# A fused decoder step on one Trainium2 core: the input projection of blocks 2 to 4 in products of 512, and a closer step distance in the last block

## The chip, the cores and the metric

The kernel runs on one core of one Trainium2 chip. The core has a matrix engine (TensorE: PE, with its weight load PEld), a vector engine (VectorE: DVE), a scalar engine (ScalarE: ACT), GpSimd (POOL), a queue engine that only issues transfers (SyncE: SP), and 16 DMA engines between main memory and the on-chip memory. PE writes its results into PSUM banks of 128 partitions by 512 fp32 columns. The metric is device time in microseconds, as a median over runs.

## The reference, cut to what matters

One layer of a decoder: 2048 prompt tokens and 64 sampled tokens pass a shared input projection, two groups of attention heads (FoX and mLSTM), an output projection and an MLP. The change is in the prompt's part of the first line:

```python
z = jnp.einsum('bsd,dc->bsc', x, w_in)          # 2112 tokens, 1024 -> 3600 columns
fq, fk, fv = z[..., 0:512], z[..., 512:1024], z[..., 1024:1536]      # FoX q, k, v
conv = conv_b + sum(xpad[:, j:j + S] * conv_w[j] for j in range(4))  # over the mLSTM q and k columns
mv, og = ..., jax.nn.sigmoid(z[..., OFF_M_O:] + b_og)                # mLSTM v and output gate
(C, n, m), h = lax.scan(_mlstm_chunk, init, chunks of q, k, v, gates)
```

All matrices are fp32. The kernel splits each operand into a high part in the PE's fp32r format and a low remainder, and forms each product as high x high, low x high and high x low.

## The kernel before, in words

**Phases.** Phase A is the input projection (about 0 to 875 us in the profile) with the mLSTM recurrence and a part of the sampled tokens' attention beside it. Phase B is the FoX attention of the prompt, phase O the output projection, phase C the MLP.

**Blocks.** Phase A goes through four blocks of tokens (`BLKS`): block 1 has the 64 sampled tokens and prompt tiles 0 to 3, blocks 2 to 4 have four tiles of 128 tokens each. In the code they are `bi` 0 to 3. A block's x, transposed to 8 slices (k) of 128 model dimensions by tokens, is split by `x_turn` into the tiles `xh0`, `xl0` (the first 256 or 320 tokens) and `xh1`, `xl1` (the last 256). `block_a(bi)` then runs five stages in this order:

- mLSTM v: `natural` twice, 256 columns of `w_in` at a time. For each tile, 24 products (`mm3` for 8 values of k: three products each) with 128 tokens as the stationary operand and 256 columns of weights as the moving one.
- mLSTM q and k, with the short convolution: 8 groups (j) of 128 columns. The weights are stationary, the tokens move: two PSUM banks (i), 24 products of 256 tokens each, and ACT copies each bank into `qi`.
- output gate: `natural` twice, the gate formed in `sink`, stored to `dog`.
- FoX q and k: 8 groups of two banks, as for mLSTM q and k, each half stored through a tile `st`.
- FoX v: `natural` twice, stored to `v_prompt`. In between, `turn_first` loads the next block's x, and splits its first tile ahead of the last tile's products of this block. In block 4 `begin_b` loads the first keys and queries of phase B.

Weights come by `wload`: for each 256 columns two transfers of 512 KB, split by ACT (high part, `whi`) and DVE (low part, `wlo`).

**What runs beside.** After each tile or bank the code calls `tick(us)`, which adds the stated time to two counters. As soon as `macc` holds more than `PACE_M` = 2.3 us, one step of the recurrence (`m_block`, for block 1's sampled tokens `m_sample`) is issued; as soon as `acc` holds more than `PACE_A` = 5.6 us, one step of the sampled attention. A step of `m_block` is a few small products with the DVE, ACT and POOL work on their results, which the next step needs. What is left of the recurrence after block 4 is issued at the end of phase A, in a loop. A framework then places every instruction in its engine's queue by its own estimate of times, so the order on an engine differs a little from that of the code.

**Names.** `pm` is the projection's PSUM tile (4 banks), `mm` and `mn` those of the recurrence, `sQ`, `sT`, `sO` those of the sampled attention, `pS` the scores of phase B. `kn`, `qn`, `nl`, `vn` are phase B's keys, queries, forget sums and values, `ks` the split keys, `wr<-w_o` the output projection's weights, which phase B asks for ahead of phase O.

Of the kernel before, what the change touches and what calls it, by code (L numbers as in the profile page):

```python
# [10 lines left out]
F32 = mybir.dt.float32  # L11
# [3 lines left out]
OP = mybir.AluOpType  # L15
# [6 lines left out]
PACE_B = float('inf')  # L22
PACE_C = 4.93
PACE_M = 2.3
D = 1024
S = 2048
NB = 8
# [25 lines left out]
def body(ctx, tc, I, O, stages):  # L53
# [99 lines left out]
    def split_hi(dst, src, scale=1.0):  # L153
        last["ACT"] = A.activation(dst, src, AF.Copy, scale=scale)  # L154

    def split_lo(dst, src, hi, eng=None):
        r = (eng or V).tensor_tensor(dst, src, hi.bitcast(F32), op=OP.subtract)  # L157
        if eng is None:
            last["DVE"] = r
        return r  # L160
# [133 lines left out]
    v_out = lambda t: (O["v_sample"].rearrange("l b t h d -> (l b t) (h d)") if t == 16  # L294
                       else O["v_prompt"].rearrange("l b s h d -> (l b s) (h d)")[t * 128:(t + 1) * 128])

    xT = {}

    def geom(bi):
        blk = BLKS[bi]  # L300
        pre = 64 if bi == 0 else 0
        off = {}
        o = 0
        for t in blk:
            off[t] = o
            o += tok_n(t)
        return blk, pre, off
# [8 lines left out]

    def x_turn(bi, t):

        blk, pre, off = geom(bi)
        i = int(off[t] >= pre + 256)  # L320
        if len(xT.setdefault(bi, [])) == i:
            w = 256 if i else 320
            xT[bi].append((pa.tile([128, 8, w], F32R, name=f"xh{i}"), pa.tile([128, 8, w], F32R, name=f"xl{i}")))
        n = tok_n(t)
        xn = xns.pop(t)[:, :8 * n].rearrange("p (k c) -> p k c", k=8)
        (xh, xl), s = xcol(bi, t)
        split_hi(xh[:, :, s], xn)
        split_lo(xl[:, :, s], xn, xh[:, :, s])

    def xcol(bi, t):  # L330

        blk, pre, off = geom(bi)
        o = off[t]
        i = int(o >= pre + 256)
        o -= i * (pre + 256)
        return xT[bi][i], slice(o, o + tok_n(t))

    def gate_stream(bi):
        blk, pre, off = geom(bi)
# [118 lines left out]
    def block_a(bi):  # L458
# [3 lines left out]
        def natural(sink, *cols, hook=None, after=None):  # L462
            wh, wl = W0.pop() if W0 else wload(*cols)
            for i, t in enumerate(blk):
                if hook:
                    hook(i)
                m = tok_n(t)
                ps = ppa.tile([128, 512], F32, name="pm", tag="pm", bufs=4)[:m, :wh[0].shape[1]]
                (xh, xl), s = xcol(bi, t)
                for k in range(8):  # L470
                    mm3(ps, xh[:, k, s], xl[:, k, s], wh[k], wl[k], k == 0, k == 7)
                sink(t, m, ps)
                if after:
                    after(i)
                tick(2.6)

        def stage(ps, m, n):
            st = pa.tile([128, 256], F32, name="st", bufs=4)[:m, :n]
# [25 lines left out]
        for j in range(8):  # L504
            if j % 2 == 0:
                wh, wl = wload((C_QK + j * 128, 256))
            cs = slice((j % 2) * 128, (j % 2) * 128 + 128)
            qi = pa.tile([128, 515], F32, name="qi", bufs=2)
            V.tensor_copy(qi[:, 0:3], hist[:, j])
            if pre:  # L510
                qs = pa.tile([128, 8, 11], F32, name="qs", bufs=2)
                V.tensor_copy(qs[:, :, 0:3], scT[:, j])
            for i in range(2):
                xh, xl = xT[bi][i]
                w = 256 + (pre if i == 0 else 0)
# [6 lines left out]
                A.copy(qi[:, 3 + i * 256:259 + i * 256], ps[:, w - 256:])  # L522
# [24 lines left out]
        if bi == 3:  # L547
            SY.dma_start(O["conv_prompt"], hist)
        yield 1
        for i in range(2):  # L550
            def sink(t, m, ps, i=i):
                r = tok_r(t)
                cs = slice(i * 256, (i + 1) * 256)
                st = pa.tile([128, 256], F32, name="st", bufs=4)[:m]
                V.tensor_tensor(st, ps, bog[:m, cs], op=OP.add)
                A.activation(st, st, AF.Tanh, scale=0.5)
                V.scalar_tensor_tensor(st, st, 1.0, nwh[:m, cs], op0=OP.add, op1=OP.mult)
                SY.dma_start(dog[r:r + m, cs], st)
            natural(sink, (C_O + i * 256, 256))
        gated.add(bi)  # L560

        for j in range(8):
# [7 lines left out]
            for i in range(2):  # L570
                xh, xl = xT[bi][i]
                w = 256 + (pre if i == 0 else 0)
                ps = ppa.tile([128, 512], F32, name="pm", tag="pm", bufs=4)[:, :w]
                for k in range(8):
                    mm3(ps, wh[k][:, cs], wl[k][:, cs], xh[:, k, :w], xl[:, k, :w], k == 0, k == 7)
                tick(w * 0.01)
                if w == 320:
                    for a in range(4):
                        V.tensor_scalar(qr[:, :, (j % 2) * 4 + a], ps[a * 32:a * 32 + 32, 0:64].rearrange("p (b t) -> p b t", t=8), scale, None, op0=OP.mult)
# [4 lines left out]
                st = pa.tile([128, 256], F32, name="st", bufs=4)  # L584
                A.activation(st, ps[:, w - 256:], AF.Copy, scale=scale)
                a = t0 + i * 256
                SY.dma_start(O["k_prompt"][jj * 128:(jj + 1) * 128, a:a + 256] if c else dq[jj, :, a:a + 256], st)
# [3 lines left out]
        for i in range(2):  # L591
            def sink(t, m, ps, i=i):
                d = v_out(t)[:, i * 256:(i + 1) * 256]
                (A if bi == 3 and i == 1 else SY).dma_start(d, stage(ps, m, 256))
# [9 lines left out]
            def b_first(n, i=i):  # L604
                if i == 1 and n == 0:
                    begin_b()
            natural(sink, (1024 + i * 256, 256), hook=b_first if bi == 3 else turn_first)

    dgs_s = drm.tile([4, 8], F32, name="dgs_s")

# [1392 lines left out]
```

## Time and profile before

| | |
|---|---|
| median of 3 runs | 3212.57 us (3210.7 to 3214.76) |
| the profiled execution's own time | 3215.55 us |
| its span, first to last instruction | 3213.8 us |
| PE busy, share of the span | 3124.1 us, 97% |
| DVE, ACT, POOL busy | 2082.2, 1446.8, 910.1 us |
| mean granted TensorE clock | 0.990 |
| DMA packets, mean | 732.75 MB, 228 GB/s |

Busy time is the union of an engine's instructions. A matmul's end is modelled and consecutive matmuls overlap, so a product's own duration is longer than the step to the next one; the step is read from the starts in the timeline. "Idle before" is the time an engine stood still just before an instruction, and the releaser is what ended it.

### The profile page before, as it was taken

What the parts mean: (1) busy time and instruction counts of PE and PEld (TensorE: products, weight loads), DVE (VectorE), ACT (ScalarE), POOL (GpSimd) and SP (SyncE); (2) the same over time, 40 slices, a digit from 0 to 9 for tenths busy, and PEclk for the clock granted to TensorE, in tenths of its full rate; (3) what the DMA queues carried; (4) which work ended last, traced back from release to release, by engine and by line L of the source; (5) the groups of instructions that cost most, each with busy time, mean ns of one, the idle gap of its engine ahead of it and who ended that gap; (6) DMA issues with size and microseconds to landing.
All of it is one profiled execution on the core that took longest, in us unless ns stands there. A gap on an engine that the chain in (4) does not pass through costs nothing. (4 is left out here: it accounts for less than half of the span.)

```text
span 3213.8 us, 57419 instructions
## 1 busy us (share of the span) xinstructions
PE 3124.1 (97%) x21597; PEld 2538.6 (79%) x21597; DVE 2082.2 (65%) x5046; ACT 1446.8 (45%) x2678; POOL 910.1 (28%) x973
## 2 busy tenths in 40 slices
PE   9999999999999999999999999999999999899998
PEld 8998998998867677677777777777767777698886
DVE  6856556465488788534556568556675665766667
ACT  4343344334378677412444445343444444344442
POOL 0121323423333333376333323334333211000000
PEclk9999999999999999999999999999999999999999
DMA  5565766867676866687887869878879866643231
GB/s 190 151 211 166 264 218 226 273 219 260 219 251 186 193 168 145 214 297 259 308 292 271 308 237 322 317 256 313 291 260 340 288 210 204 211 163 131 100 123 63
DMA packets 339340, 732.75 MB, mean 228 GB/s; under 512 B 63608, under 2 KB 177656, under 8 KB 338168
## 3 DMA queue, kind: packets, MB, share of 16 engines
q1 hardware_dynamic: 251928, 414.61, 39.8%
q0 software_dynamic: 83520, 304.12, 27.1%
q10 hardware_dynamic: 3616, 10.36, 0.9%
q8 instruction: 171, 2.80, 0.3%
q14 instruction: 105, 0.86, 0.1%
HBM read 676.13 MB, written 86.38 MB: 237 GB/s over the span
## 5 line engine op out<-in xcount | busy, mean ns | idle before, releaser
L157 DVE TENSOR_TENSOR wl<-wr,wh 128x1024 fp32r<-128x1024 f32 x300 | 365.7, 1222 | 246.1 <-ACT wh L154 207.1
L154 ACT ACTIVATE wh<-wr 128x1024 fp32r<-128x1024 f32 x300 | 315.4, 1055 | 330.7 <-PE py L165 140.0
L163 PE MATMUL ph<-x1h,wh 128*128 128x512 f32 (+1 forms) x1280 | 455.2, 356 | 0.0
L164 PE MATMUL ph<-x1l,wh 128*128 128x512 f32 (+1 forms) x1280 | 453.5, 354 | 0.2 <-DVE x1l L157 0.2
L165 PE MATMUL ph<-x1h,wl 128*128 128x512 f32 (+1 forms) x1280 | 451.5, 355 | 0.4 <-DVE wl L157 0.2
L1720 POOL DMA_INDIRECT kT<-cache_k,idxK x256 | 276.4, 1080 | 533.7 <-PE sQ L1743 468.6
L163 PE MATMUL py<-wh,hh 128*128 128x512 f32 x900 | 358.8, 403 | 10.4 <-DVE y L1369 6.4
L164 PE MATMUL py<-wl,hh 128*128 128x512 f32 x900 | 354.4, 395 | 0.7 <-issue 0.7
L165 PE MATMUL py<-wh,hl 128*128 128x512 f32 x900 | 351.9, 395 | 0.7 <-DVE hl L157 0.4
L1369 DVE TENSOR_TENSOR y<-y,py 128x512 f32<-128x512 f32 x410 | 276.8, 681 | 106.5 <-PE py L165 80.3
L163 PE MATMUL pm<-xh,whi 128*128 128x256 f32 (+1 forms) x1024 | 298.5, 292 | 0.0
L164 PE MATMUL pm<-xl,whi 128*128 128x256 f32 (+1 forms) x1024 | 294.5, 288 | 0.0
L165 PE MATMUL pm<-xh,wlo 128*128 128x256 f32 (+1 forms) x1024 | 293.6, 287 | 0.5 <-issue 0.5
L1831 POOL DMA_INDIRECT vt<-cache_v,idxV x164 | 179.1, 1092 | 386.8 <-PE sO L1855 315.1
L163 PEld LDWEIGHTS ph<-x1h,wh 128*128 128x128 f32 x1280 | 241.2, 188 | 40.2 <-issue 8.5
L165 PEld LDWEIGHTS ph<-x1h,wl 128*128 128x128 f32 x1280 | 240.6, 189 | 36.7 <-issue 3.7
L164 PEld LDWEIGHTS ph<-x1l,wh 128*128 128x128 f32 x1280 | 241.5, 189 | 35.0 <-issue 3.7
L163 PE MATMUL pm<-whi,xh 128*128 128x256 f32 (+2 forms) x816 | 237.0, 291 | 9.8 <-ACT whi L154 7.2
L164 PE MATMUL pm<-wlo,xh 128*128 128x256 f32 (+2 forms) x816 | 232.6, 285 | 0.8 <-DVE wlo L157 0.6
L165 PE MATMUL pm<-whi,xl 128*128 128x256 f32 (+2 forms) x816 | 232.3, 285 | 0.8 <-issue 0.8
L163 PEld LDWEIGHTS py<-wh,hh 128*128 128x128 f32 x900 | 169.4, 189 | 65.2 <-issue 25.1
L157 DVE TENSOR_TENSOR wlo<-wra,whi 128x1024 fp32r<-128x1024 f32 (+1 forms) x112 | 141.6, 1266 | 102.0 <-ACT whi L154 95.5
(364 smaller groups left out, 6806.7 us busy)
## 6 DMA issues: line engine op xcount, KB each, us to landing
wr<-w SPq DMA_DIRECT2D x200, 512.0 KB
wra<-w_in SPq DMA_DIRECT2D x104, 512.0 KB
wr<-dw SPq DMA_DIRECT2D x96, 512.0 KB
dw<-w POOLq DMA_DIRECT2D x48, 512.0 KB
Rb<-dR SPq DMA_DIRECT2D x128, 128.0 KB
kT<-dw SPq DMA_DIRECT2D x28, 512.0 KB
kT<-w SPq DMA_DIRECT2D x25, 512.0 KB
xn<-xp_t SPq DMA_DIRECT2D x16, 512.0 KB
```

The source lines that it names most:

```text
L154: last["ACT"] = A.activation(dst, src, AF.Copy, scale=scale)
L157: r = (eng or V).tensor_tensor(dst, src, hi.bitcast(F32), op=OP.subtract)
L163: T.matmul(ps, wh, xh, start=first, stop=False, skip_group_check=shared)
L164: T.matmul(ps, wh, xl, start=False, stop=False, skip_group_check=shared)
L165: last["PE"] = T.matmul(ps, wl, xh, start=False, stop=stop, skip_group_check=shared)
L1369: V.tensor_tensor(y, y, ps, op=op)
L1720: G.indirect_dma_start(out=piece(n), out_offset=None, in_=ck, in_offset=IO(ap=idxK[:, b, j // 2, j % 2:j % 2 + 1], axis=0))
L1831: vx["last"] = G.indirect_dma_start(out=vt.rearrange("p f c -> p (f c)"), out_offset=None, in_=cv, in_offset=IO(ap=idxV[:, b, (kt % 4) * 4 ...
```

## The change

In blocks 2 to 4 a block's x lies in one pair of tiles `XX` (`xh`, `xl`, 4608 columns), tile by tile, each tile as 8 slices of 128 tokens. mLSTM q and k and FoX q and k take all 512 tokens of a block in one product, whose moving operand is then four runs of 128 tokens. Output gate and FoX v are formed by a new function `wide`: four PSUM banks are open at once, one for each tile, the weights come in four pieces q of 2 slices by 512 columns, and each product moves 512 columns, as two runs of 256 with a step between them. mLSTM v and all of block 1 stay as they were. The ticks of the two kinds of stages add up to the same. In block 4 `PACE_M` becomes 2.05 us after the output gate. FoX v of block 4 is stored from the ACT queue for all four tiles.

```diff
+PACE_M3 = 2.05
...
-    xT = {}
+    XX = []
...
     def x_turn(bi, t):
-        blk, pre, off = geom(bi)
-        i = int(off[t] >= pre + 256)
-        if len(xT.setdefault(bi, [])) == i:
-            w = 256 if i else 320
-            xT[bi].append((pa.tile([128, 8, w], F32R, name=f"xh{i}"), pa.tile([128, 8, w], F32R, name=f"xl{i}")))
+        if not XX:
+            XX.extend(pa.tile([128, 4608], F32R, name=x) for x in ("xh", "xl"))
...
+    def xrun(bi):
+        if bi:
+            return [(512, [X[:, 0:4096].rearrange("p (t k c) -> p k t c", t=4, k=8) for X in XX])]
+        return [(w, [X[:, a:a + 8 * w].rearrange("p (k c) -> p k c", k=8) for X in XX]) for a, w in ((0, 320), (2560, 256))]
...
+        def wide(sink, c0, hook=None):
+            banks = [ppa.tile([128, 512], F32, name="pm", tag="pm", bufs=4) for _ in blk]
+            at0, at1 = (w_at[((c0 + i * 256, 256),)] for i in range(2))
+            for q in range(4):
+                wr = pa.tile([128, 4 * 272], F32, name="wra", bufs=2)[:, :1024]
+                SY.dma_start(wr.rearrange("p (s e) -> p s e", s=2),
+                             dap(I["w_in"], at0 + q // 2 * 131072 + q % 2 * 512, [[1024, 128], [at1 - at0, 2], [1, 512]]))
...
+                split_hi(wh, wr)
+                split_lo(wl, wr, wh)
+                wh, wl = (x.rearrange("p (s k c) -> p k s c", s=2, k=2) for x in (wh, wl))
+                for i, t in enumerate(blk):
+                    xh, xl = xcol(bi, t)
+                    for k in range(2):
+                        mm3(banks[i].rearrange("p (s c) -> p s c", s=2), xh[:, 2 * q + k], xl[:, 2 * q + k], wh[:, k], wl[:, k],
+                            q == k == 0, q == 3 and k == 1)
+                    if hook:
+                        hook(q, i)
+                    if q == 3:
+                        st = (pa.tile([128, 512], F32, name="sa", tag="ac", bufs=2) if i % 2 else
+                              pa.tile([128, 512], F32, name="sq", tag="qi", bufs=2))
+                        sink(t, banks[i], st)
+                    tick(1.3)
...
-            for i in range(2):
-                xh, xl = xT[bi][i]
-                w = 256 + (pre if i == 0 else 0)
+            for w, (xh, xl) in xrun(bi):
                 ps = ppa.tile([128, 512], F32, name="pm", tag="pm", bufs=4)[:, :w]
+                pv = ps.rearrange("p (t c) -> p t c", t=4) if w == 512 else ps
                 for k in range(8):
-                    mm3(ps, wh[k][:, cs], wl[k][:, cs], xh[:, k, :w], xl[:, k, :w], k == 0, k == 7)
+                    mm3(pv, wh[k][:, cs], wl[k][:, cs], xh[:, k], xl[:, k], k == 0, k == 7)
                 tick(w * 0.01)
...
+        if bi == 3:
+            macc[2] = PACE_M3
...
+        def at(q, i):
+            if bi == 3:
+                if (q, i) == (2, 0):
+                    begin_b()
+            elif q < 3 and i == 0:
+                x_load(BLKS[bi + 1][q])
+            elif (q, i) == (3, 0):
+                x_turn(bi + 1, BLKS[bi + 1][0])
+                x_load(BLKS[bi + 1][3])
+
+        if bi:
+            wide(v_store, 1024, at)
```

Three places show what stands in the queues. The first is PE among block 4's FoX q groups, where half a step of the recurrence (`mn`, products of chunk values `va` and state `Cs`) stands between the projection's products (`pm`). Before, at the change from the first half of the block's tokens (`xh0`, `xl0`) to the second (`xh1`, `xl1`):

```order
L164 MATMUL pm_10094<-xl0_8442,whi_9976 128x256
L165 MATMUL pm_10094<-xh0_8441,wlo_9977 128x256
L719 MATMUL mn_10119<-va_9576,Wm_9579 128x129
L720 MATMUL mn_10119<-Cs_8404,qa_9581 128x129
L719 MATMUL mn_10119<-va_9576,Wm_9579 128x129
L720 MATMUL mn_10119<-Cs_8404,qa_9581 128x129
L163 MATMUL pm_10138<-xh1_8512,whi_9970 128x256
L164 MATMUL pm_10138<-xl1_8513,whi_9970 128x256
```

After, at the change from one group of 128 columns to the next (the tiles `xh` and `xl` hold all 512 tokens):

```order
L165 MATMUL pm_8447<-xl_148,whi_8354 128x512
L166 MATMUL pm_8447<-xh_147,wlo_8355 128x512
L778 MATMUL mn_8472<-va_8089,Wm_8092 128x129
L779 MATMUL mn_8472<-Cs_7119,qa_8094 128x129
L778 MATMUL mn_8472<-va_8089,Wm_8092 128x129
L779 MATMUL mn_8472<-Cs_7119,qa_8094 128x129
L778 MATMUL mn_8483<-va_8089,Wm_8092 128x129
L779 MATMUL mn_8483<-Cs_7119,qa_8094 128x129
L778 MATMUL mn_8483<-va_8089,Wm_8092 128x129
L779 MATMUL mn_8483<-Cs_7119,qa_8094 128x129
L164 MATMUL pm_8548<-xh_147,whi_8538 128x512
L165 MATMUL pm_8548<-xl_148,whi_8538 128x512
```

Each group of 24 products of 256 has become part of one of 24 products of 512, and two steps (the two `mn` halves) now stand together where before one stood, with 24 products of 256 between it and the next.

The second place is PE at the end of phase A: the last products of FoX v in block 4, the last of the recurrence (`mn<-va,kw`, and the transposes `mm<-ident,hh` of its result), and the first scores of phase B (`pS`). Before:

```order
L163 MATMUL pm<-whi,xh_8512 128x256
L164 MATMUL pm<-wlo,xh_8512 128x256
L165 MATMUL pm<-whi,xl_8513 128x256
L728 MATMUL mn<-va,kw 128x129 x4
L634 MATMUL mm<-ident,hh 128x128 x4
L974 MATMUL pS<-ks_11274,qh 128x256
L975 MATMUL pS<-ks_11274,ql 128x256
L974 MATMUL pS<-ks_11274,qh 128x256
```

After:

```order
L164 MATMUL pm<-whi,xh 128x512
L165 MATMUL pm<-wlo,xh 128x512
L166 MATMUL pm<-whi,xl 128x512
L693 MATMUL mm<-ident,hh 128x128 x4
L164 MATMUL pm<-whi,xh 128x512
L165 MATMUL pm<-wlo,xh 128x512
L166 MATMUL pm<-whi,xl 128x512
L164 MATMUL pm<-whi,xh 128x512
L165 MATMUL pm<-wlo,xh 128x512
L166 MATMUL pm<-whi,xl 128x512
L1033 MATMUL pS<-ks_9340,qh 128x256
L1034 MATMUL pS<-ks_9340,ql 128x256
```

The transposes stood behind the last product of the projection; now six products of 512 stand behind them, and the last `mn` products stand earlier still.

The third place is the SP queue at the same end, where the results of the recurrence (`C_prompt`, `n_prompt`, `dmix`) and phase B's first loads are issued. Before:

```order
L637 DMA dmix<-ot 128x4x128
L925 DMA nl_11273<-dnl 128x512
L926 DMA vn_11272<-v_prompt 128x4x64
L741 DMA C_prompt<-Cs 128x4x128
L931 DMA kn<-k_prompt 64x512
L744 DMA n_prompt<-nn 128x4
L931 DMA kn<-k_prompt 64x512
L637 DMA dmix<-ot 128x4x128
L925 DMA nl_11273<-dnl 128x512
L926 DMA vn_11272<-v_prompt 128x4x64
L949 DMA qn<-dq 64x256 x4
```

After:

```order
L800 DMA C_prompt<-Cs 128x4x128
L803 DMA n_prompt<-nn 128x4
L696 DMA dmix<-ot 128x4x128
L1197 DMA wr<-w_o 128x1024 x3
L984 DMA nl_9339<-dnl 128x512
L985 DMA vn_9338<-v_prompt 128x4x64
L990 DMA kn<-k_prompt 64x512 x2
L984 DMA nl_9339<-dnl 128x512
L985 DMA vn_9338<-v_prompt 128x4x64
L1008 DMA qn<-dq 64x256 x4
L990 DMA kn<-k_prompt 64x512 x2
```

The first loads of `nl` and `vn` stood ahead of `C_prompt`; now they stand behind it and behind three loads of the output projection's weights (`wr<-w_o`, 512 KB each), which before came some sixty issues later.

More of the change, by code (lines that the diff above doesn't have):

```diff
@@ L475, in natural @@
                 tick(2.6)
+        def wide(sink, c0, hook=None):
[5 more added lines that the diff above has]
+                             dap(I["w_in"], at0 + q // 2 * 131072 + q % 2 * 512, [[1024, 128], [at1 - at0, 2], [1, 512]]))
+                wh = pa.tile([128, 4 * 272], F32R, name="whi", bufs=4)[:, :1024]
+                wl = pa.tile([128, 4 * 272], F32R, name="wlo", bufs=4)[:, :1024]
+                split_hi(wh, wr)
+                split_lo(wl, wr, wh)
+                wh, wl = (x.rearrange("p (s k c) -> p k s c", s=2, k=2) for x in (wh, wl))
+                for i, t in enumerate(blk):
+                    xh, xl = xcol(bi, t)
+                    for k in range(2):
[8 more added lines that the diff above has]
+                    tick(1.3)
         def stage(ps, m, n):
@@ L549, in block_a, with gate_out @@
         yield 1
-        for i in range(2):
+        def gate_out(t, ps, st):
+            V.tensor_tensor(st, ps, bog, op=OP.add)
+            A.activation(st, st, AF.Tanh, scale=0.5)
+            V.scalar_tensor_tensor(st, st, 1.0, nwh, op0=OP.add, op1=OP.mult)
+            SY.dma_start(dog[t * 128:t * 128 + 128], st)
+        if bi:
+            wide(gate_out, C_O)
+        for i in range(0 if bi else 2):
             def sink(t, m, ps, i=i):
@@ L583, in block_a @@
                         SY.dma_start(O["k_sample"][jj * 128:(jj + 1) * 128], st)
[L584 to L587, printed above, removed]
+                for o in range(w % 256, w, 256):
+                    st = pa.tile([128, 256], F32, name="st", bufs=4)
+                    A.activation(st, ps[:, o:o + 256], AF.Copy, scale=scale)
+                    SY.dma_start(O["k_prompt"][jj * 128:(jj + 1) * 128, a:a + 256] if c else dq[jj, :, a:a + 256], st)
+                    a += 256
             if pre and j % 2 == 1:
@@ L590, in block_a, with v_store @@
         kx["new"] = True
-        for i in range(2):
+        def v_store(t, ps, st):
+            A.copy(st, ps)
+            (A if bi == 3 else SY).dma_start(v_out(t), st)
+        def at(q, i):
[7 more added lines that the diff above has]
+                x_load(BLKS[bi + 1][3])
+        if bi:
+            wide(v_store, 1024, at)
+        for i in range(0 if bi else 2):
             def sink(t, m, ps, i=i):
-                d = v_out(t)[:, i * 256:(i + 1) * 256]
-                (A if bi == 3 and i == 1 else SY).dma_start(d, stage(ps, m, 256))
+                SY.dma_start(v_out(t)[:, i * 256:(i + 1) * 256], stage(ps, m, 256))
             def turn_first(n, i=i):
@@ L602, in turn_first @@
                     x_load(BLKS[bi + 1][3])
[L604 to L607, printed above, removed]
+            natural(sink, (1024 + i * 256, 256), hook=turn_first)
     dgs_s = drm.tile([4, 8], F32, name="dgs_s")
```

36 lines of the change are left out of this document (20 added, 16 removed).

## The prediction

> **What bounds the kernel now.** I read the page first, then busy time by stage, then what PE waited for in phase A. The first fence is the span and the busy times of the page; the second has three windows that cover blocks 2 to 4 (start:end, length, then busy time and instructions of PE, PEld, DVE, ACT, POOL, the clock, the DMA share and GB/s); the third is the two longest of PE's waits between 245 and 900 us.
>
> ```profile
> span 3213.8 us, 57419 instructions
> PE 3124.1 (97%) x21597; PEld 2538.6 (79%) x21597; DVE 2082.2 (65%) x5046; ACT 1446.8 (45%) x2678; POOL 910.1 (28%) x973
> ```
>
> ```profile
> 245.00:450.00 205.00, 205.00 (x1750) 188.33 (x1750) 127.01 (x370) 73.11 (x147) 52.20 (x52) 1.00 0.67 215
> 450.00:660.00 210.00, 204.47 (x1890) 190.74 (x1889) 117.92 (x343) 80.43 (x178) 71.24 (x72) 1.00 0.72 237
> 660.00:880.00 220.00, 213.84 (x1991) 198.55 (x1989) 119.99 (x342) 80.68 (x178) 74.28 (x82) 1.00 0.71 239
> ```
>
> ```profile
> PE sO L1855 <- DMA vt<-cache_v,idxV: 3.2, 2, 2.7
> PE mm L634 <- DVE pad_4x L85: 2.5, 1, 2.5
> ```
>
> PE is busy for 623.3 of these 635 us, at full clock; DVE is at 57%, ACT at 37%, DMA at 0.7. So in blocks 2 to 4 time is what PE's products take one after the other. What the change saves on PE here shortens the kernel, unless it brings a new wait.
>
> **What a product costs.** A busy time hides this, since products overlap; the step between two starts tells it. First a run of 256-column products in phase A, then a run of 512-column products in phase C, each by its first and last row.
>
> ```profile
> 700.60 0.28 PE L165 MATMUL pm<-xh,wlo 128*128 128x256 f32 x1
> ...
> 703.12 0.28 PE L165 MATMUL pm<-xh,wlo 128*128 128x256 f32 x1
> ```
>
> ```profile
> 2104.75 0.40 PE L165 MATMUL ph<-x1h,wl 128*128 128x512 f32 x1
> ...
> 2107.03 0.39 PE L163 MATMUL py<-wh,hh 128*128 128x512 f32 x1
> ...
> 2110.43 0.39 PE L163 MATMUL py<-wh,hh 128*128 128x512 f32 x1
> ```
>
> The first has 21 steps in 2.52 us, 0.1200 each. The second has 25 steps in 5.68 us, 0.2272 each: 0.228 over its first ten, 0.2267 over its last fifteen. Two products of 256 take 0.2400, one of 512 takes 0.2272: 0.0128 us saved for each pair that becomes one. Here rows and the Trainium skill differ. Its page TensorE: Matmul & The Clock Gate ("Wait — 56ns, not 53.3ns?") gives a warm product N/2.4 GHz plus about 2.5 ns, so that a pair would save 2.5 ns and the change some 4 us (an estimate from that page). The trace has 120 ns where that rule has 109, so the rows decide.
>
> **The sum, part by part.**
>
> *Fewer products.* In each of blocks 2 to 4: mLSTM q and k, 8 groups x 2 halves x 24 products become 8 x 24, 192 fewer; FoX q and k likewise 192; gate and FoX v, 4 tiles x 2 x 24 become 4 x 24, 96 fewer each. That is 576 a block, 1728 in all. 1728 x 0.0128 = 22.1 us; by the ends of the 512 run, 20.7 (0.228) to 23.0 (0.2267). I take 22. Weight loads fall by as many, and they lie beside products (PEld 79%).
>
> *Operands in several runs.* The 512 moving columns are four runs of 128 in 1152 products and two of 256 in 576: 1152 x 3 + 576 = 4032 joints. No projection product of before has one. The nearest row is the sampled attention, whose keys (`kT`) move as two runs of 128, while its values (`vt`) move as one run of 256:
>
> ```profile
> 2450.68 1.07 PE L1743 MATMUL sQ<-kT,qb 128*32 128x256 f32 x16
> ...
> 2456.70 1.07 PE L1855 MATMUL sO<-vt,PTs 128*32 128x256 f32 x16
> ```
>
> Both take 1.07 us for 16. I cost a joint at nothing; these are products of another form, so a small price could hide in them, and more than nothing is the first rival. No gain is possible here. The Trainium skill speaks against this edit: Advanced Engine Details and Errata has, under PSUM's cachelines, that any non-contiguous access pattern significantly slows matmuls. The result tiles stay contiguous here; only the reading side gets joints.
>
> *Evacuation and stores.* Four pairs of gate additions, activations and stores of 256 columns a block become four of 512, off PE's path. All four banks are held through a `wide`, and the next stage's first bank was emptied by the copy of the tile that ended 18 products (4.1 us) earlier. What that copy takes is at most 0.58 us on ACT (row L636 below). I cost it at nothing, at 0.5 us a stage, 3 us in all, if the cover fails.
>
> *The next block's x.* The split of a block's first tile was beside 24 products of 256 (2.9 us); now it may begin when tile 0's last products end, with 18 products of 512 (4.1 us) left. It is one row of each:
>
> ```profile
> L157 DVE TENSOR_TENSOR xl<-xn,xh 128x1024 fp32r<-128x1024 f32 x8 | 9.6, 1220 | 0.0
> L154 ACT ACTIVATE xh<-xn 128x1024 fp32r<-128x1024 f32 x8 | 8.0, 1052 | 5.6 <-PE pm L164 5.6
> ```
>
> 1.05 + 1.22 = 2.3 us, covered. The later tiles follow on ACT with one copy between, still within the 2.9 us that each tile of mLSTM v lasts. Nothing; 2 x 2.3 = 4.6 us if uncovered both times.
>
> *The end of phase A.* Rows of PE, ACT and DVE around it (start, length):
>
> ```profile
> 875.08 0.28 PE L165 MATMUL pm<-whi,xl 128*128 128x256 f32 x1
> 875.20 1.05 PE L728 MATMUL mn<-va,kw 128*128 128x129 f32 x8
> 878.74 0.77 PE L634 MATMUL mm<-ident,hh 128*128 128x128 f32 x4 [2.49 <-DVE pad_4x L85]
> 880.44 0.58 PE L974 MATMUL pS<-ks,qh 128*128 128x256 f32 x1 [0.93 <-DVE ks L157]
> ```
>
> ```profile
> 875.80 0.34 ACTq L594 DMA_DIRECT2D v_prompt<-st  x1
> 876.24 0.42 ACT L154 ACTIVATE qh<-qn 128x256 fp32r<-128x256 f32 x1 [0.47 <-ACT st L479]
> 876.56 0.61 ACT L154 ACTIVATE ks<-kn 128x512 fp32r<-128x512 f32 x1
> 879.55 0.58 ACT L636 COPY ot<-mm 128x512 f32<-128x512 f32 x1 [2.37 <-PE mm L634]
> ```
>
> ```profile
> 879.48 0.90 DVE L157 TENSOR_TENSOR ks<-kn,ks 64x512 fp32r<-64x512 f32 x1
> ```
>
> From the last projection product to the first `pS` are 5.36 us. The recurrence's last products and its DVE chain stand in them, and DVE splits `ks` only at 879.48 though ACT was done at 877.17. At 2.05 us a step instead of 2.3, the order has all of the recurrence ahead of the last six products, so after them only this is left: a product (0.4), the copy of 512 columns (0.58), the store's issue (0.34), `qh` and `ks` on ACT (0.32 + 0.61), `ks` on DVE (0.90), with gaps 3.4 us. PE gains 2.0.
>
> But the SP queue gives some back. Its rows before, and a window while the output projection's weights arrive:
>
> ```profile
> 869.10 0.33 SPq L925 DMA_DIRECT2D nl<-dnl  x1
> ...
> 878.02 0.39 SPq L741 DMA_DIRECT2D C_prompt<-Cs  x1
> ...
> 882.16 2.49 SPq L949 DMA_DIRECT2D qn<-dq  x4
> ...
> 920.96 2.71 SPq L1138 DMA_DIRECT2D wr<-w_o  x5
> ```
>
> ```profile
> 925.00:930.00 5.00, 5.00 (x36) 2.86 (x35) 3.79 (x15) 4.43 (x10) 0.46 (x1) 1.00 1.01 403
> ```
>
> Before, `C_prompt` held the queue for the recurrence until 878.02, and the `qn` of phase B's second unit went out at 882.16, 7.1 us after the last product. Now `C_prompt` finds its data early, but three loads of 512 KB stand ahead of `nl`, `vn`, `kn` and `qn`: 1.6 us of issue (0.54 each), and 1.57 MB at 403 GB/s, 3.9 us. The second of the three has a wait for PE; queued behind it are those four, and POOL's `nd<-nl`, DVE's first scores and ACT's `qh` wait for them. `nl`, which lay ready before, then lands about 6.5 us after the last product (2 until its issue, 3.9 behind the weights, 0.65 for its own 256 KB, an estimate), 3.1 after the first scores could start; `qn` lands about when it did. So the gain of 2.0 lies between 3 (the earlier `C_prompt` counts in full) and -4 (the loads count in full); I take 1.
>
> *The steps' distance* itself costs nothing: it moves the same steps. Two steps at a tick are the third rival. Fewer products leave less cover for the gathers behind the 3.2 us wait on `vt`; I expect a few tenths more and no term.
>
> Sum: 22 + 1 = 23 us off. The profiled execution took 3215.55 us, 1.75 beyond its span; 23 less is a span of 3190.8 and 3192.5 in all. The median of the runs shown, 3212.57, lies 2.98 below the profiled one, so I give 3189.6, rounded **3190**. A measurement of this kernel tells about 0.2% (6.4 us) from no change.
>
> **The rivals.**
>
> *Joints cost (slower).* If PE needs time at each joint, the place is every 512 product of phase A. It decides from 23 / 4032 = 5.7 ns a joint. At 10 ns, about what 24 columns take ((0.2272 - 0.1200) / 256 us a column), it costs 40 us: 3190 + 40 = 3230. For it: no fp32r product of before has joints. Against: the two 1.07 us rows, in which 10 ns a joint would show even with four products side by side. The rule on access patterns named above would end here. Chance 0.06.
>
> *The fixed cost is not saved.* A step of 256 is 13 ns longer than its columns at (0.2272 - 0.1200) / 256 us each; if that part belongs to the columns of this operand, tile or format rather than to the instruction, a 512 step in phase A is 0.240 and only the end's 1 us is left: 3211.6, no change. Against: the 512 run of phase C, in the same format. The rule of 2.5 ns a product from the skill's page on the clock gate would come near to it. Chance 0.05.
>
> *Paired steps stall PE.* A group of 512 tokens ticks 5.12 us at once and releases two steps. The second needs the first's results on DVE and ACT: from the last product of a half step to its `hh`,
>
> ```profile
> 868.59 0.39 PE L720 MATMUL mn<-Cs,qa 128*128 128x129 f32 x2
> 869.68 0.63 ACT L651 ACTIVATE hh<-mn,dn 128x128 f32<-128x128 f32 x2 [1.43 <-DVE dn L649]
> ```
>
> 1.7 us. FoX q and k tick 8 times in each of three blocks: 24 x 1.7 = 41 us at most, if the order put dependent steps side by side. It mostly does not: it moves projection products between them (the two halves that stand together in the first place shown don't depend on each other). At a third of it 14 us come back: 3204, still faster by more than 0.2%. Chance 0.11, of which 0.02 at two thirds (28 us, 3218), on the edge of slower.
>
> **Chances.** The forecast has 0.78, between 3183 (all terms at their good ends, 23 + 3, and 4 us less waiting than before) and 3198 (20.7 - 4, the copies' and splits' 7.6 partly). The range 3181 to 3205 adds the milder part of the third rival and holds some 0.8. Faster by over 0.2%: 0.78 + 0.09 = 0.87. Within: 0.05 + 0.01 = 0.06. Slower: 0.06 + 0.01 = 0.07.
>
> **What would show it.** In the changed profile: products of 512 in phase A at a step of 0.227 to 0.228 (right), 0.23 to 0.25 (a joint or a fixed cost); phase B's first `pS` about 24 us earlier; the first `pS` 3 to 4 us after the last `pm`, and the waits after it on `nl` and `qn` longer or not; PE's waits on `mn` and `mm` products in blocks 2 to 4 still a few us together; the phases after unchanged in length. PE idle of over 15 us in blocks 2 to 4, or a step above 0.234, would prove the forecast wrong.

## The result, and the profile after

The changed kernel takes 3229.48 us (median of 5, 3228.69 to 3242.08); before takes 3214.76 us in runs beside it (median of 5, 3210.7 to 3219.37). The ratio is 1.0055, 95% interval 1.0042 to 1.0069: slower by some 15 to 18 us, where the forecast had 23 us less. The profiled execution took 3232.28 us against 3215.55.

The page's span and busy times, then blocks 2 to 4 in three windows (length, busy time and instructions of PE, PEld, DVE, ACT, POOL, the granted clock, DMA share, GB/s):

```profile
span 3230.5 us, 53788 instructions
PE 3114.2 (96%) x19869; PEld 2447.7 (76%) x19869; DVE 2085.1 (65%) x5022; ACT 1439.3 (45%) x2630; POOL 902.2 (28%) x973
```

```profile
245.00:450.00 205.00, 199.19 (x1120) 154.56 (x1119) 117.18 (x325) 66.04 (x120) 43.06 (x46) 0.99 0.64 210
450.00:660.00 210.00, 200.76 (x1326) 161.51 (x1326) 122.37 (x343) 76.87 (x167) 74.86 (x77) 0.99 0.70 238
660.00:896.00 236.00, 223.74 (x1504) 176.74 (x1501) 126.31 (x365) 84.03 (x172) 75.56 (x81) 0.98 0.69 230
```

PE stands idle for 27 us here, against 12 in the windows of before, and the clock, which was 1.00, is 0.98 to 0.99. The waits that PE had between 128 and 897 us (total, times, longest), the longest six:

```profile
PE sO L1914 <- DMA vt<-cache_v,idxV: 5.0, 2, 3.9
PE sT L1871 <- ACT PTs L1873: 4.6, 1, 4.6
PE mm L693 <- POOL hh L688: 4.5, 4, 1.7
PE mr L386 <- DVE rows L393: 3.3, 1, 3.3
PE pS L1033 <- DVE ks L158: 2.9, 1, 2.9
PE mm L693 <- POOL va L722: 2.7, 1, 2.7
```

All but the `pS` row are waits of the recurrence (its gates, `mr`, among them) or of the sampled attention, each of them long and rare, and released by four different engines or queues.

The products themselves do what was forecast. First and last row of a run of 24 in block 4's mLSTM q and k, whose operand is four runs of 128:

```profile
704.01 0.39 PE L166 MATMUL pm<-xh,wlo 128*128 128x512 f32 x1
...
709.22 0.39 PE L165 MATMUL pm<-xl,whi 128*128 128x512 f32 x1
```

23 steps in 5.21 us are 0.2265 each: no price for a joint.

**A wait costs twice.** Four windows around the 4.6 us wait, and a row of products behind it:

```profile
650.00:652.00 2.00, 0.00 (x0) 0.00 (x0) 0.00 (x0) 1.15 (x4) 0.00 (x0) 1.00 0.30 113
652.00:654.00 2.00, 1.13 (x5) 1.14 (x6) 0.20 (x1) 1.77 (x4) 1.73 (x3) 0.57 0.01 4
654.00:656.00 2.00, 2.00 (x6) 1.57 (x6) 1.92 (x3) 0.00 (x0) 2.00 (x3) 0.57 0.00 0
656.00:658.00 2.00, 1.83 (x10) 1.27 (x10) 0.53 (x3) 1.12 (x3) 0.57 (x1) 1.00 0.18 25
```

```profile
654.21 0.63 PE L164 MATMUL pm<-whi,xh 128*128 128x512 f32 x1
654.63 0.63 PE L165 MATMUL pm<-wlo,xh 128*128 128x512 f32 x1
655.06 0.63 PE L166 MATMUL pm<-whi,xl 128*128 128x512 f32 x1
```

For 4 us after it the granted clock is 0.57, and a product takes 0.43 us instead of 0.227: another 1.4 us. Phase A has six such stretches (from 133, 208, 423, 652, 717 and 820 us), before none; at 1.4 to 2.6 us each, lowered clock times PE's busy time, they cost about 10 us. The first two lie in block 1, whose products are as before. e7 below, whose products stand in the same order on PE in phase A, shows neither in its profile, but the other four at the same places; e2's, in the same order until block 4's FoX q and k, shows the second, third and last. So some come and go with the execution.

**The bill of the profiled execution.** The last product of phase A starts at 893.25 instead of 875.1, and the first `pS` at 896.54 instead of 880.44: 16 us later. The 1728 saved pairs give about -17 (below), the end of phase A -2. PE's waits up to its last product are some 18 us more, its wait for the first weights 1, the lowered clock some 10; 6 us more are spread over small steps and not apportioned. Then the start of phase B loses 6.7: from the first `pS` to the first `pw` 444.5 us, before 437.8. The phases behind it take 6 us less in this execution. Profiles of one kernel differ by some us a stage (the executions above by 13 in all), so the verdicts below rest on medians; where profiles are compared, it is on sums.

### The profile page after: what moved, and what is told of

It reads as the page before. It is cut to its first block, busy times and chain, and to the rows that moved or that the text cites. A ratio compares the mean times of both kernels' runs of the same rounds, so it can differ in the third digit from the quotient of the medians.

```text
span 3230.5 us, 53788 instructions
## 1 busy us (share of the span) xinstructions
PE 3114.2 (96%) x19869; PEld 2447.7 (76%) x19869; DVE 2085.1 (65%) x5022; ACT 1439.3 (45%) x2630; POOL 902.2 (28%) x973
## 5 line engine op out<-in xcount | busy, mean ns | idle before, releaser
L164 PE MATMUL pm<-xh,whi 128*128 128x512 f32 (+2 forms) x640 | 231.8, 362 | 0.0
L166 PE MATMUL pm<-xh,wlo 128*128 128x512 f32 (+2 forms) x640 | 229.2, 358 | 0.0
L165 PE MATMUL pm<-xl,whi 128*128 128x512 f32 (+2 forms) x640 | 228.2, 357 | 0.0
L164 PEld LDWEIGHTS py<-wh,hh 128*128 128x128 f32 x900 | 169.0, 189 | 60.3 <-issue 20.8
L164 PE MATMUL pm<-whi,xh 128*128 128x256 f32 (+4 forms) x624 | 204.4, 329 | 10.0 <-ACT whi L155 8.0
L165 PE MATMUL pm<-wlo,xh 128*128 128x256 f32 (+4 forms) x624 | 201.6, 323 | 0.6 <-DVE wlo L158 0.6
L166 PE MATMUL pm<-whi,xl 128*128 128x256 f32 (+4 forms) x624 | 201.2, 323 | 0.4 <-DVE xl L158 0.4
```

The costliest lines, as they stand in the source:

```text
L164: T.matmul(ps, wh, xh, start=first, stop=False, skip_group_check=shared)
L165: T.matmul(ps, wh, xl, start=False, stop=False, skip_group_check=shared)
L166: last["PE"] = T.matmul(ps, wl, xh, start=False, stop=stop, skip_group_check=shared)
```

## The experiments

Five edits recur. *Halves*: the column groups of blocks 2 to 4 in two products of 256 tokens, from the same tiles.

```diff
-            return [(512, [X[:, 0:4096].rearrange("p (t k c) -> p k t c", t=4, k=8) for X in XX])]
+            return [(256, [X[:, a:a + 2048].rearrange("p (t k c) -> p k t c", t=2, k=8) for X in XX]) for a in (0, 2048)]
```

*Natural*: gate and FoX v in two passes of 256 columns as before (the gate's lines; those of FoX v are cut here).

```diff
-        if bi:
-            wide(gate_out, C_O)
-        for i in range(0 if bi else 2):
+        for i in range(2):
```

*Hold*: the four `w_o` loads wait for the products of phase B's sixth step (the lines of `half_wo` that add the dependency are cut here).

```diff
+            if n == 6:
+                held = last["PE"].ins.name
             if n == 60:
-                wo.extend(half_wo(0, q) for q in range(4))
+                wo.extend(half_wo(0, q, held) for q in range(4))
```

*Split*: a 512-token group calls its step budget in two halves. *Scaled*: the budgets of the 512 stages go down to what their products now take.

```diff
+                    if w == 512 and k == 3:
+                        tick(2.56)
-                tick(w * 0.01)
+                tick(w * 0.01 if w < 512 else 2.56)
```

```diff
-                tick(w * 0.01)
+                tick(w * (0.0095 if w == 512 else 0.01))
-                    tick(1.3)
+                    tick(1.23)
```

All ratios are to the kernel before on the same chip. PE idle is 600 us less PE's busy time in the window 260 to 860 us, from one profile each. It counts less than the ratio: a profiled execution can lie far from its kernel's median (e5's took 3228.78 us against 3214.29, e12's 3200.84 against 3209.25).

| kernel | ratio (95%) | PE idle, us |
|---|---|---|
| before | 1 | 8.7 |
| changed | 1.0055 (1.0042 to 1.0069) | 23.4 |
| e2 old distance | 1.0033 (1.0020 to 1.0046) | 22.3 |
| e7 hold | 1.0038 (1.0022 to 1.0054) | 22.1 |
| e4 wide only (halves) | 1.0003 (0.9991 to 1.0015) | 6.6 |
| e10 wide only, hold | 0.9968 (0.9957 to 0.9980) | 5.1 |
| e14 the same, scaled | 0.9969 (0.9955 to 0.9983) | 8.0 |
| e8 wide only, old distance | 0.9972 (0.9960 to 0.9984) | 5.0 |
| e5 layout only (halves, natural), hold | 1.0006 (0.9993 to 1.0019) | 10.4 |
| e16 before with closer steps, hold | 1.0013 (0.9998 to 1.0027) | 10.2 |
| e3 columns only (natural) | 1.0025 (1.0012 to 1.0039) | 16.2 |
| e20 wide, mLSTM q and k at 512, hold | 0.9996 (0.9985 to 1.0008) | 10.5 |
| e22 the same, scaled | 1.0023 (1.0012 to 1.0033) | 19.4 |
| e21 wide, FoX q and k at 512, hold | 1.0045 (1.0028 to 1.0063) | 17.4 |
| e1 split | 1.0025 (1.0014 to 1.0037) | 15.7 |
| e9 scaled, hold | 0.9995 (0.9983 to 1.0007) | 15.2 |
| e12 split, scaled, hold | 0.9992 (0.9978 to 1.0007) | 15.2 |
| e15 scaled to 0.0090 and 1.17, hold | 1.0003 (0.9991 to 1.0015) | 15.3 |
| e17 recurrence's budget scaled, hold | 1.0017 (1.0004 to 1.0030) | 24.1 |
| e18 sampled attention's budget scaled, hold | 1.0004 (0.9990 to 1.0017) | 20.8 |

### Where in phase A: the wide stages or the column groups

e4 is *halves*, e3 is *natural*, e5 is both with *hold*.

> The changed kernel with gate and FoX v of blocks 2 to 4 at 512 columns (576 products, 7.4 us saved) but the column groups in two products of 256 tokens, one step budget of 2.56 us each as before. Paired steps: the waits go, 3213 + 8 - 7 = about 3214 us. Wide stages: the waits stay and the columns' 15 us are lost too, about 3244. Start of phase B: 3214. Lost cover: 3215 to 3225.

> The changed kernel with 512 tokens in the column groups (QK, FoX q and k of blocks 2 to 4: 1152 products, 14.7 us saved at 0.0128 us a pair) but gate and FoX v in two passes of 256 columns as before. Paired steps: the waits stay, 3229 + 7 = about 3236 us. Wide stages: the waits go, only the 8 us at the start of phase B are left, about 3213 + 8 - 15 = 3206. Start of phase B: as wide, if the order at the end is unchanged. Lost cover: 3215 to 3230.

> The new layout of x alone (one pair of tiles, tile by tile), every product at 256 columns as before, the column groups' operand as two runs of 128 tokens; last block's steps at 2.05 us, w_o loads held. If the layout and its joints cost nothing, the tail's 2 us are all that is left: ratio 0.999 to 1.000, products at a step of 0.120 us. If the shared pair of x tiles or the joints are what costs phase A its waits: 1.004 or more.

The window 260 to 860 us of e4 with the loads held (e10), of before and of the changed kernel:

```profile
260.00:860.00 600.00, 594.90 (x4852) 523.13 (x4852) 351.55 (x987) 223.93 (x464) 194.15 (x194) 1.00 0.70 234
```

```profile
260.00:860.00 600.00, 591.29 (x5347) 547.34 (x5346) 351.44 (x997) 225.41 (x483) 190.61 (x194) 1.00 0.70 232
```

```profile
260.00:860.00 600.00, 576.60 (x3612) 453.99 (x3610) 344.99 (x956) 214.79 (x430) 180.09 (x187) 0.99 0.69 233
```

The layout with its joints costs nothing measurable. With wide stages alone PE idles no more than before. With the columns alone it idles 16 us and is slower than before, though e3 saves twice the products that e4 does. So the new waits come with the 512-token column groups. The theory "wide stages" falls.

Where they lie is another matter. In blocks 2 to 4 of the changed kernel PE waits 10 us inside the column groups (before: 5) and 15 us in FoX v and mLSTM v, the stages behind them (before: 0.2). FoX v of block 2 with mLSTM v of block 3 lost most; before, then changed:

```profile
409.00:470.00 61.00, 61.00 (x544) 58.91 (x544) 33.16 (x110) 25.09 (x53) 23.13 (x23) 1.00 0.70 228
```

```profile
405.00:485.00 80.00, 71.43 (x500) 61.43 (x499) 45.45 (x146) 30.08 (x63) 25.96 (x31) 0.98 0.65 205
```

By the timeline 144 products of the recurrence stand there, where before had 96; block 2's three stages ahead of it have 138 instead of 185. So the order has moved recurrence work out of the column groups into the next stages, though the budgets add up to the same, and PE waits there too. e7 repeats it (80.5 us); with one column stage in halves (e20, e21) the stretch takes 61 and 64 us. The pile alone doesn't make the waits: e9, with 138 products there, waits 3 us and takes 70. Why the order comes out so was not tested.

Which of them? e20 and e21 each turn one of the two column stages back into halves, with *hold*.

> Gate, FoX v and mLSTM q and k at 512, FoX q and k in two products of 256 tokens; w_o loads held, budgets not scaled. Without the column stages at 512 this was 0.9968, with both 1.0038: 22 us lie between. If each of the two has half: 1.000. If mLSTM q and k has them (its convolution on DVE and ACT follows each group): 1.003; if FoX q and k has them: 0.994 to 0.996.

> Gate, FoX v and FoX q and k at 512, mLSTM q and k in two products of 256 tokens; w_o loads held, budgets not scaled. Half each: 1.000. If FoX q and k brings the waits: 1.003; if mLSTM q and k does: 0.994 to 0.996.

From e10, mLSTM q and k at 512 lose 9 us, FoX q and k 25, and both together (e7) 22. Each alone saves 7.4 us of products by the forecast's price, 6 by the one measured below. FoX q and k is the worse, but the shares don't add up.

### The start of phase B

e2 sets `PACE_M3` to 2.3; e7 is *hold* alone; e10 is e4 with *hold*; e8 is e4 with 2.3 and no hold.

> The changed kernel with the last block's recurrence steps at the old distance of 2.3 us instead of 2.05. Start of phase B (at 2.05 the recurrence ends before the last products and the w_o loads come ahead of nl): the wait of 9 us after the first pS falls to 1 to 3 us, but the recurrence stands behind the last product again, 5 us instead of 3; about 3222 to 3225 us. The other theories: the stages before 786 us are the same to a few tenths, 3227 to 3231 in all.

> The changed kernel with the four w_o loads that phase B asks for early held until the products of phase B's sixth step, so that nl, vn, kn and qn go first on SP. If the loads ahead of nl cost what the first comparison shows (first pS to first pw 444.5 us against 437.8 before), 6.7 us come back: the wait after the first pS falls from 9.2 to 2 to 4 us, pS to pw is about 438, and the time is 0.2% lower than the changed kernel's, some 1.003 of before. If the waits of phase B only move (DMA full whatever comes first), pS to pw stays at 443 to 445 and the ratio at 1.0055.

> Only gate and FoX v of blocks 2 to 4 at 512 columns, the column groups in two products of 256 tokens, and the w_o loads held. Run with the loads not held it was 1.0003 of before. If the start of phase B costs 6.7 us there too, this is the first version below before: about 3216 - 6 = 3210 us, ratio 0.998. If that start is not what the time goes to, 1.000.

> Only gate and FoX v of blocks 2 to 4 at 512 columns, the last block's steps at the old 2.3 us, w_o loads not held. At 2.05 this was 1.0003 with the loads ahead of nl and 0.9968 with them held. If the closer distance does nothing but bring the loads forward and take 2 us off the tail, 2 us above the held one: 0.997 to 0.998. If it has a price or a gain of its own beyond that: below 0.996 or above 0.999.

The timeline of the changed kernel at that place:

```profile
893.25 0.40 PE L166 MATMUL pm<-whi,xl 128*128 128x512 f32 x1
...
893.37 1.55 SPq L1197 DMA_DIRECT2D wr<-w_o  x3
...
894.97 0.42 SPq L984 DMA_DIRECT2D nl<-dnl  x1
...
904.50 2.10 POOL L1026 TENSOR_TENSOR nd<-nl,dmask 128x128 f32<-128x128 f32 x5 [10.36 <-DMA nl<-dnl]
...
906.14 0.47 PE L1078 MATMUL pt<-ident,S 128*128 128x128 f32 x1 [8.89 <-ACT S L1062]
```

The cleanest pair is e4 and e10, with the last product within 1 us of each other; first e4, then e10:

```profile
872.26 1.51 SPq L1197 DMA_DIRECT2D wr<-w_o  x3
...
883.49 0.47 PE L1078 MATMUL pt<-ident,S 128*128 128x128 f32 x1 [7.39 <-ACT S L1062]
```

```profile
871.24 0.56 SPq L984 DMA_DIRECT2D nl<-dnl  x1
...
876.92 0.48 PE L1078 MATMUL pt<-ident,S 128*128 128x128 f32 x1 [1.31 <-ACT S L1062]
```

The first `pt` starts 11.4 us after the last product in the one and 5.8 in the other, and the ratios are 1.0003 and 0.9968. This part of the loss is shown; of the 11 us between the ratios, 6 are seen at this place. In the changed kernel itself the hold brings a ratio of 1.0038 against 1.0055, with intervals that overlap; its wait before `pt` falls from 8.89 to 3.81 us. e8 without the closer distance has 0.9972: the distance itself does nothing beyond the tail's 2 us and the place of the loads.

### Pairs of steps, or their distance

e1 is *split*; e9 is *scaled* with *hold*; e12 is *split* (2.43 a half) with *scaled* and *hold*.

> The changed kernel, but a 512-token column group calls the step budget twice, 2.56 us after its first four and 2.56 us after its last four 128-row pieces, so one recurrence step is released at a time. Four theories share the 38 us that the change lost against its 22 us of saved product time. Paired steps (two steps released side by side at a 5.12 us tick stall TensorE): most of the 38 us are in the column stages and go, about 3207 us, and the waits of 2 to 5 us with the slow products behind them between 128 and 897 us mostly vanish. Wide stages (gate and FoX v in pieces over four held banks): 3225 to 3230. Start of phase B (w_o loads ahead of nl): 3225 to 3230, wait after the first pS still 9 us. Lost cover (any saving of product time comes back as a wait for a transfer or a slower engine): 3220 to 3230, as many waits at other places.

> As the kernel with the w_o loads held, and the step budgets of the 512 stages scaled to what the products now take (0.0095 us a column instead of 0.01, 1.23 instead of 1.3 for each piece of wide), so that a recurrence step comes after as many microseconds of PE as before. Closer steps (the products got shorter and the step distance did not): a third to two thirds of the 33 us of new waits in phase A go, 10 to 20 us below the kernel with only the loads held, ratio 0.997 to 1.000. Paired steps or other places of the order: as the kernel with the loads held, within 4 us.

> The changed kernel with w_o loads held, step budgets scaled to what the products take, and the column groups' budget called in two halves of 2.43 us. If pairing and closeness each cost their own share (the two runs before gave 8.5 us for the one and 14 us for the other), about 8 us below the run with scaled budgets alone: ratio 0.997. If both are the same waits: 0.9995 again.

Split alone takes PE's idle time from 23 to 16 us and the ratio from 1.0055 to 1.0025, less than half of what "paired steps" asked for, with the start of phase B still bad. Scaled takes 14 us off (1.0038 to 0.9995), as "closer steps" had it. Both together are no better than scaled alone. So three more runs tested distance: e15 sets it farther (0.0090 and 1.17), e16 puts closer steps into the kernel before, e14 scales the wide-only version.

```diff
 # e16, in the kernel before
-                tick(w * 0.01)
+                tick(w * (0.01056 if bi else 0.01))
-                tick(2.6)
+                tick(2.75 if bi and cols[0][0] in (C_O, C_O + 256, 1024, 1280) else 2.6)
```

> The changed kernel with w_o loads held and the step budgets of the 512 stages at 0.0090 a column and 1.17 a piece, 5% farther apart in PE time than before. If the distance sets the waits, they fall on: 4 to 8 us below the run at 0.0095, ratio 0.997 to 0.998, unless steps of the recurrence are left over at the end of phase A, where each costs its 2 us bare. If 0.0095 only happened to fall well: 1.002 to 1.004.

> The kernel before, all products of 256 columns, with the step budgets of the same stages of blocks 2 to 4 raised by 5.6% (0.01056 a column, 2.75 instead of 2.6 for a tile of the gate and of FoX v), so that the recurrence's and the sampled attention's steps come as close in PE time as in the changed kernel, but no product is saved; w_o loads held. Closer steps: new waits of PE in phase A, 12 to 30 us, ratio 1.004 to 1.009. If the new waits belong to the 512 form (a whole bank at once, later evacuation, paired steps): within 3 us of before, ratio 0.999 to 1.001.

> Only gate and FoX v at 512 columns, w_o loads held, and the budget of wide's pieces scaled to 1.23. With the budget at 1.3 this was 0.9968. In that run PE's waits in phase A were no longer than before, so closeness costs it little: 0.996 to 0.998.

e16 loses 4 us (0 to 9), not the 12 to 30 that "closer steps" needed. e15 has its last product at 863.2 us, 6 earlier than e9, but the first `pS` only at 889.3: the steps left over run bare for 26 us. e14 gains nothing. Then one stream at a time, and the scaled budgets for e20:

```diff
 # e17; e18 has the two arguments the other way round
-                tick(w * 0.01)
+                tick(w * (0.0095 if w == 512 else 0.01), w * 0.01)
```

> The changed kernel with w_o loads held, where in the 512 stages only the recurrence's budget is scaled (0.0095 a column, 1.23 a piece); the sampled attention's stays at 0.01 and 1.3. If the recurrence's distance makes the waits: as with both scaled, ratio 0.999 to 1.000. If the sampled attention's does: 1.003 to 1.004, as with the loads held alone. If each has a share: 1.001 to 1.002.

> The counterpart: only the sampled attention's budget is scaled, the recurrence's stays. If the recurrence's distance makes the waits: 1.003 to 1.004. If the sampled attention's does: 0.999 to 1.000.

> Gate, FoX v and mLSTM q and k at 512, FoX q and k in two products of 256; step budgets of the 512 stages scaled (0.0095 and 1.23), w_o loads held. Not scaled this was 0.9996, without the q and k groups 0.9968. If the step distance is what mLSTM q and k lost by, its 7 us of saved products now count: 0.995. If not: 0.999.

e17 and e18 each get part of the 14 us, 7 and 11 by the ratios, with intervals that overlap those around them. e22 goes the other way: scaled, e20's ratio rises from 0.9996 to 1.0023. Its window, and those of e20 and e9:

```profile
260.00:860.00 600.00, 580.60 (x4206) 486.46 (x4206) 350.98 (x967) 217.66 (x435) 185.56 (x190) 0.99 0.69 228
```

```profile
260.00:860.00 600.00, 589.55 (x4311) 494.73 (x4310) 352.75 (x993) 221.15 (x443) 186.00 (x194) 1.00 0.70 234
```

```profile
260.00:860.00 600.00, 584.80 (x3681) 464.95 (x3683) 353.31 (x982) 216.61 (x439) 184.96 (x191) 0.99 0.68 229
```

A budget that helps the one version by 14 us hurts the other by 9. Distance as the cause falls too: it moves the waits, up or down.

### How such a wait comes about

The chain in front of the 3.9 us wait for `vt` in the changed kernel:

```profile
800.82 0.38 SPq L715 DMA_DIRECT2D Wm<-dM  x1
...
807.57 1.28 ACT L747 ACTIVATE Wm<-Wm,gm 128x128 f32<-128x128 f32 x4 [4.75 <-DMA Wm<-dM]
...
808.92 0.64 POOL L748 TENSOR_SCALAR_AFFINE_SELECT Wm<-Wm 128x512 f32<-128x512 f32 x1 [4.21 <-ACT Wm L747]
...
810.89 1.27 POOL L688 TENSOR_TENSOR hh<-hh,og 128x512 f32<-128x512 f32 x1
...
813.69 0.95 POOL L1890 DMA_INDIRECT vt<-cache_v,idxV  x1 [0.30 <-issue]
...
821.16 1.93 PE L1914 MATMUL sO<-vt,PTs 128*32 128x256 f32 x16 [3.88 <-DMA vt<-cache_v,idxV]
```

The recurrence's load lands 6.7 us after its issue. ACT stands idle 4.75 us for it and POOL 4.21 us behind ACT, and POOL issues the other stream's gather behind that, which arrives 7.5 us later. ACT's waits for this load between 128 and 874 us (total, times, longest), before and changed:

```profile
ACT Wm L688 <- DMA Wm<-dM: 36.8, 12, 5.4
```

```profile
ACT Wm L747 <- DMA Wm<-dM: 62.5, 13, 9.5
```

That a late load of one stream holds up both is read from these rows; no run took it away. **Settled**: the loss has two places. One is PE's waits in phase A with the slow products behind them; they come with the column groups of 512 tokens, and lie in the changed kernel partly in them and for the larger part in the stages behind them. The other is the `w_o` loads ahead of `nl`. **Open**: why a 512-token group brings such waits and a wide stage does not. Pairing explains part in one version and nothing in another, distance part in one and the reverse in another, either stream part in the one version where it was tried. No run kept PE's order as it was in before while the products grew to 512.

### A version that beats both

e10, wide stages only with the loads held: 3204.09 us (median of 12), before 3213.63 beside it, ratio 0.9968 (0.9957 to 0.9980). Its 576 pairs are some 6 us at the measured price and the tail 2; the rest of the 10 lies within the interval (6 to 14 us).

## Why the prediction was wrong, by its own steps

- **Fewer products: mechanism right, term too large.** The step is 0.2265 as forecast. But over the whole of blocks 2 to 4, waits and stretches of lowered clock left out, the step that starts at a projection product of 256 averages 0.1235 us in e10, that of a product of 512 in e12 0.2369: 0.0101 us a pair, not 0.0128, since steps around other products and the odd longer one are in it. For 1728 pairs that is 17 us, not 22.
- **Joints cost nothing: right** (0.2265, and e5). The rule on access patterns from the Trainium skill's page Advanced Engine Details and Errata (PSUM Cachelines), which the prediction set aside, is not borne out for the operand that is read; the result tiles stayed contiguous, so no run here shows it for them.
- **Evacuation, held banks, the next block's x: right.** The waits on them that the changed kernel's profile shows are 0.4 us in all in blocks 2 to 4, and e10's gain, 6 to 14 us, has room for the wide stages' whole share.
- **End of phase A: half right.** The first `pS` comes 3.29 us after the last product (forecast 3.4). But SP's share was sized wrong: `nl` was to land 6.5 us after the last product and landed by 904.50, 11.3 after it. I counted 1.57 MB of weights and 256 KB ahead of it. By the windows, of which the first and last of six follow, 3.4 MB were moved by then (length times GB/s, summed), so loads issued behind `nl` moved beside it:

```profile
893.40:895.50 2.10, 0.25 (x2) 0.00 (x0) 0.37 (x2) 1.35 (x3) 0.43 (x3) 1.00 0.99 280
...
903.50:904.50 1.00, 0.00 (x0) 0.00 (x0) 0.00 (x0) 0.00 (x0) 0.00 (x1) 0.50 0.61 163
```

  The term +1 should have been 2 less 6.7.
- **The step that failed: PE's waits.** The sum took PE as the bound, and its waits beside the projection as unchanged, "a few tenths more and no term". They grew by 18 us, and the clock behind them took 10 more. With PE idle for 27 us in blocks 2 to 4 the forecast's own sign of being wrong (over 15) is met. Why the waits grew so stays open, as said above.
- **The third rival was the nearest, and underpriced.** Paired steps were given 14 us and a chance of 0.11, with no price at all for the slow products behind a wait. Its 41 us counted FoX q and k alone, though mLSTM q and k tick alike and lost 9 us (e20). Nor is pairing the mechanism: undoing it took 9 us off in one version and none in another. "It mostly does not: it moves projection products between them" took the order of the products for a guarantee of time.
- **The clock.** At 1.00 in all three windows of before, it had no term. The Trainium skill's page TensorE: Matmul & The Clock Gate (HAM oscillation — how this bites in real kernels) says that a gap of over about 3.4 us returns PE to half clock. The trace agrees for the 4.6 us wait (0.57), but has lowered clocks behind waits of 1.8 to 2.7 us as well (last section).

## What to carry to other kernels

When the bounding engine gets faster, its cover for everything beside it gets thinner: price the forecast's saving against new waits, one stage at a time, and try the stages singly, since here a third of the saved products gained 10 us and the rest lost 22. Ask of every work stream that ends earlier which loads it lets go first, and who stands behind them. Tuning the distance of side work by one number is a search, not a rule: 0.0095 for 0.01 was worth -14 us in one version and +9 in another.

## What the runs showed of the hardware that was not expected

A wait shorter than 3.4 us can lower the clock, and of two short waits the longer need not. The windows from 206 us and from 442.6 us of the changed kernel, around waits of 2.1 and 2.0 us, and what followed:

```profile
206.00:208.00 2.00, 0.09 (x1) 0.00 (x0) 0.57 (x1) 1.11 (x4) 1.40 (x3) 1.00 0.53 136
208.00:210.00 2.00, 1.82 (x10) 1.83 (x11) 1.11 (x5) 0.00 (x0) 0.00 (x0) 0.64 1.04 343
210.00:212.00 2.00, 2.00 (x12) 2.00 (x11) 0.13 (x1) 0.00 (x0) 0.00 (x0) 0.51 1.05 327
```

```profile
442.60:445.00 2.40, 0.41 (x4) 0.22 (x3) 0.41 (x2) 1.68 (x6) 0.00 (x0) 1.00 0.91 347
445.00:447.00 2.00, 2.00 (x18) 2.00 (x19) 0.80 (x4) 2.00 (x5) 1.71 (x3) 1.00 0.47 183
```

The first is followed by 4 us at 0.64 and 0.51, the second by full clock. The wait of 1.85 us that ends at 131.99 is followed, from 133 us on, by 3.4 us at half clock; the one of 2.66 us in before that ends at 539.08 by none. So in these traces the length of a wait below 3 us does not tell whether the clock falls.
